# Projections of a hybrid attention and SSD layer in column-tile pairs by seven products (Strassen's scheme), token halves in turn, V in four pieces

## The chip, the cores and the metric

The kernel runs on one core of a Trainium2 chip, written in Bass with the Tile framework. The metric is the device time of one execution in microseconds (us). The engines are named as in the profile: PE (TensorE, matmuls), PEld (its weight loads), DVE (VectorE), ACT (ScalarE), POOL (GpSimd) and SP (SyncE, which here only issues DMAs).

## The reference, cut to what matters

One decoder layer over 2048 tokens of 1024 channels, in float32. One input projection feeds two branches: dilated sliding-window attention with three dilations, and a Mamba-2 SSD mixer behind a causal convolution of width 4.

```python
proj = jnp.einsum('bsd,de->bse', x, w_in[layer])          # 2048 x 1024 times 1024 x 6672
q, k, v, z_att, z_ssm, xbc, dt_raw = jnp.split(proj, list(SPLITS), axis=-1)
# three dilated windows over q, k, v, merged by their log-sum-exps
y_att = rms_norm(y_att.reshape(Bsz, S, D_ATT) * jax.nn.silu(z_att), att_norm_g[layer])
xbc = jax.nn.silu(causal_depthwise_conv(xbc, conv_w[layer], conv_b[layer]))
xs, bm, cm = jnp.split(xbc, [D_SSM, D_SSM + SSM_GROUPS * SSM_STATE], axis=-1)
# chunked scan of 16 chunks of 128 tokens over xs, bm, cm, dt
y_ssm = rms_norm(y.reshape(Bsz, S, D_SSM).astype(x.dtype) * jax.nn.silu(z_ssm), ssm_norm_g[layer])
out = jnp.einsum('bse,ed->bsd', jnp.concatenate([y_att, y_ssm], axis=-1), w_out[layer])
x = layer_norm(alpha * x + out, ln_g[layer], ln_b[layer])
```

## The kernel before, in words

Every large product keeps float32 accuracy by a split of both factors into a high part (float32r) and a low rest, and three matmuls: high times high, high times low, low times high. The split of x is made once: `load_x` brings a tile of 128 channels by 1024 tokens, ACT copies it to `xh`, DVE subtracts to get `xl`. The 32 tiles of xh and xl (8 channel blocks k, 2 token halves i, high and low) stay in SBUF through the whole first half of the kernel.

V comes first (L154 to L156). Here the tokens are the output's partitions and the columns run along the free axis, in pieces of 384, 384 and 272 columns (the last holds the 16 columns of dt as well). `load_v` loads and splits the weights of a piece, `v_out` evacuates the PSUM tile of 128 tokens into `vt` (two buffers) and stores it to DRAM in three layouts, `d_v[0]` to `d_v[2]`, one for each dilation. The first piece runs with the channel blocks outermost on eight PSUM tiles, so that it can begin while x is coming in; the other two run tile by tile, each after a column tile of z.

The rest of the projection has 44 column tiles of 128 columns, where the columns are the partitions and 512 tokens the free axis. `proj(ct, fin)` loads a tile's weights (`load_w`, split by ACT and POOL), and for each of four blocks of 512 tokens makes 8 x 3 matmuls into one PSUM tile (L111 to L113), then calls `fin`, which evacuates it: `fin_z` (SiLU, to `d_za`), `fin_qk` (high and low parts to `d_qh`, `d_ql`, `d_kh`, `d_kl`), `fin_zs` (SiLU of the SSM gate, to `d_zs`) or `conv_evac` into a tile U of all 2048 tokens, from which `conv_out` makes the convolution on DVE (L227, L229), its SiLU on ACT (L233) and the stores to `d_xs` and `d_bc`. The order: V with two tiles of z, 12 convolution tiles, the decays (dt), 8 tiles of the SSM gate with `split_w` beside them (the output weights scaled by the norm's gains, split and stored to `d_wo`), then 16 tiles of q and k and the last z tiles. Beside the q and k tiles run the 32 units of the SSD scan, `ssd(n, g)`: 16 chunks by 2 groups.

After that come attention (eight pairs of heads, on an order written out by hand) and the output projection with both norms; both read what the first half stored to DRAM. The order of instructions on each engine in the first half is made when the kernel is built, by a list scheduler with a simulated timeline; on the chip each engine takes its instructions in that order. All of SP's DMAs stand in one queue, POOL's in another. Pools opened after others were closed reuse their memory, and a tile there waits until the tiles that it overlaps are done with.

Of the kernel before, what the change touches and what calls it, by code (L numbers as in the profile page):

```python
# [9 lines left out]
F32 = mybir.dt.float32  # L10
# [18 lines left out]
def hybrid_layer(ctx, tc, xT, xc, w52, wv, convw, convb, dtb, alog, dskp, gcol, wout,  # L29
# [23 lines left out]
    d_zs = [dtile(f"d_zs{g}", [16, 128, 4, 128]) for g in range(2)]  # L53
# [21 lines left out]

    with ExitStack() as c1:
        xp = c1.enter_context(tc.tile_pool(name="xp", bufs=1))
        wp = c1.enter_context(tc.tile_pool(name="wp", bufs=2))
        ev = c1.enter_context(tc.tile_pool(name="ev", bufs=5))
        sm = c1.enter_context(tc.tile_pool(name="sm", bufs=1))  # L80
        pp = c1.enter_context(tc.tile_pool(name="pp", bufs=3, space=PSUM))
        ss = c1.enter_context(tc.tile_pool(name="ss", bufs=5, space=PSUM))
# [6 lines left out]
        xh, xl = [[None, None] for k in range(8)], [[None, None] for k in range(8)]  # L89
        for i in range(2):  # L90
            for k in range(8):
                xh[k][i] = xp.tile([128, 1024], F32R, name=f"xh{k}_{i}")
                xl[k][i] = xp.tile([128, 1024], F32R, name=f"xl{k}_{i}")

        def load_w(ct):
            raw = wp.tile([128, 8, 128], F32, name="wraw")
            nc.sync.dma_start(raw, w52[ct])
            hi = wp.tile([128, 8, 128], F32R, name="whi")
            lo = wp.tile([128, 8, 128], F32R, name="wlo")
            nc.scalar.copy(hi, raw)  # L100
            nc.gpsimd.tensor_tensor(lo, raw, hi.bitcast(F32), op=OP.subtract)  # L101
            return hi, lo

        def proj(ct, fin, w=None, tbs=range(4)):
            hi, lo = w or load_w(ct)
            for tb in tbs:
                ps = pp.tile([128, 512], F32, name="pp")
                s = slice(tb % 2 * 512, tb % 2 * 512 + 512)
                for k in range(8):
                    h, l = xh[k][tb // 2][:, s], xl[k][tb // 2][:, s]  # L110
                    nc.tensor.matmul(ps, hi[:, k, :], h, start=(k == 0), stop=False)  # L111
                    nc.tensor.matmul(ps, hi[:, k, :], l, start=False, stop=False)  # L112
                    nc.tensor.matmul(ps, lo[:, k, :], h, start=False, stop=(k == 7))  # L113
                fin(ps, tb)

        def fin_z(i):
            def f(ps, tb):
                e = ev.tile([128, 512], F32, name="ev")
                nc.scalar.activation(e, ps, AF.Silu)
                nc.sync.dma_start(d_za[i][:, tb * 512:tb * 512 + 512], e)  # L120
            return f

        def fin_qk(i, scale):
            def f(ps, tb):
                hi = ev.tile([128, 512], F32R, name="ev")
                lo = ev.tile([128, 512], F32, name="ev")
                nc.scalar.activation(hi, ps, AF.Copy, scale=scale)
                nc.vector.scalar_tensor_tensor(lo, ps, scale, hi.bitcast(F32), op0=OP.mult,
                                               op1=OP.subtract)
                s = slice(tb * 512, tb * 512 + 512)  # L130
                dh, dl = (d_kh, d_kl) if scale == 1.0 else (d_qh, d_ql)
                nc.sync.dma_start(dh[i][:, s], hi.bitcast(F32))
                nc.sync.dma_start(dl[i][:, s], lo)
            return f


        with tc.tile_pool(name="vp", bufs=1, reuse_waits="tile") as vp:
            vw = {}
            COLS = ((0, 384), (384, 384), (768, 272))

            def load_v(pc, k):
                c0, w = COLS[pc]
                vh, vl = [vp.tile([128, 384], F32R, name=f"v{p}{k}")[:, 0:w] for p in "hl"]
                raw = vp.tile([128, 384], F32, name="vraw", bufs=2)[:, 0:w]
# [13 lines left out]
            vts = {}  # L158

            def v_out(ps, pc, r, dtj=None):  # L160
                c0, w = COLS[pc]
                if pc == 2:
                    w = 256
                    nc.vector.tensor_copy(dtj[:, 16 * r:16 * r + 16], ps[:, w:w + 16])
                r4, s4 = r // 4, r % 4
                if s4 == 0:
                    vts[0] = vp.tile([128, 4, 384], F32, name="vt", bufs=2)[:, :, 0:w]
# [9 lines left out]
            pst = [pp.tile([128, 512], F32, name="pp") for _ in range(3)]  # L177
            pst += [ss.tile([128, 512], F32, name="ss") for _ in range(5)]

            def load_x(k, i):  # L180
                st = wp.tile([128, 1024], F32, name=("wraw", "whi", "wlo")[k % 3])
# [6 lines left out]
            for i in range(2):  # L188
                for k in range(8):
                    if i == 0:  # L190
                        load_v(0, k)
                    load_x(k, i)
                    for r in range(8):
                        v_mm(pst[r], 0, 8 * i + r, k)
                for r in range(8):
                    v_out(pst[r], 0, 8 * i + r)
            nc.sync.dma_start(ident, cst[:, 0:128])
            nc.sync.dma_start(tri, cst[:, 128:256])
            nc.sync.dma_start(cw, convw)
            nc.sync.dma_start(cb, convb)  # L200
            nc.sync.dma_start(dsk, dskp)
            nc.sync.dma_start(gc, gcol)

            for pc in (1, 2):
                proj(23 + pc, fin_z(pc - 1))
                for k in range(8):
                    load_v(pc, k)
                dtj = ev.tile([128, 512], F32, name="ev")[:, 0:256] if pc == 2 else None
                for r in range(NR):
                    ps = pp.tile([128, 512], F32, name="pp")  # L210
                    for k in range(8):
                        v_mm(ps, pc, r, k)
                    v_out(ps, pc, r, dtj)
            nc.sync.dma_start(d_dt.rearrange("j r h -> j (r h)"), dtj)


        def conv_evac(U, ps, tb):
            p3 = ps.rearrange("p (s j) -> p s j", j=NJ)
            evac(tb, U[:, 3 + tb:19:4, :], p3)
            if tb:  # L220
                nc.vector.tensor_copy(U[:, tb - 1, 1:NJ], p3[:, 3, 0:NJ - 1])
            else:
                nc.gpsimd.memset(U[:, 0:3, 0:1], 0.0)

        def conv_out(cp, U, i):
# [5 lines left out]
            o = cp.tile([128, 16, NR, 8], F32, name="cvo", bufs=1)  # L231
# [12 lines left out]
        with tc.tile_pool(name="cp", bufs=2, reuse_waits="tile") as cp:  # L244
            for i in range(12):
# [176 lines left out]
        for i in range(8):  # L422
            jobs += [(i, fin_qk(i, -0.125)), (8 + i, fin_qk(i, 1.0))]
# [538 lines left out]
```

## Time and profile before

| | |
|---|---|
| Time, median of 3 runs | 2191.73 us (2190.43 to 2192.97) |
| The profiled execution: time, span | 2193.83 us, 2192.0 us |
| Granted TensorE clock, mean over the span | 0.984 |
| Busy share of the span: PE, PEld, DVE, ACT, POOL | 98%, 81%, 53%, 39%, 38% |
| Bytes moved by DMA, mean rate | 363.66 MB, 166 GB/s |
| Hardware queue (SP's): MB, share of the 16 DMA engines | 278.45, 41.8% |
| Software queue (POOL's): MB, share of the 16 DMA engines | 82.84, 10.6% |

Matmuls are pipelined: each row of the profile gives one matmul's time from its start to its modelled end, which is longer than the distance from one start to the next. What a matmul costs in a full stretch is therefore read from the number of matmuls in a window, not from its mean duration. The rows of windows give, for each engine, its busy time and its number of instructions in that window, then the granted clock, the mean busy share of the DMA engines, and GB/s.

### The profile page before, as it was taken

How to read it: one execution, taken by the hardware profiler on the slowest of the kernel's cores; microseconds unless marked ns; L12 is line 12 of the kernel's file. 1: busy time of each engine (PE TensorE's matmuls, PEld its weight loads, DVE VectorE, ACT ScalarE, POOL GpSimd, SP SyncE). 2: the span in 40 equal slices, each digit the busy share in tenths (PEclk: the TensorE clock that was granted, in tenths of full speed). 3: DMA queues.
4: the chain of work that ended last, by engine and by line, in shares of the span. 5: the costliest groups of instructions: out<-in, count | busy, mean ns of one | idle time of the engine just before them, and what ended most of it. 6: DMA issues, size and time to landing. Idle time of an engine off the chain costs nothing.

```text
span 2192.0 us, 37071 instructions
## 1 busy us (share of the span) xinstructions
PE 2138.5 (98%) x13968; PEld 1784.6 (81%) x13968; DVE 1166.2 (53%) x2941; ACT 847.8 (39%) x2289; POOL 838.8 (38%) x589
## 2 busy tenths in 40 slices
PE   8999999999999999999999999999999976999998
PEld 8999888888888888888888878888878865888886
DVE  4000255555223555554544258888888845655655
ACT  4101122223112333232345368887888841222221
POOL 3101010102442455555555321776666670322322
PEclk9999999999999999999999979999999988999999
DMA  8644222224786656555543542777876799232220
GB/s 281 182 133 139 70 78 71 77 71 148 249 262 208 206 194 198 178 190 177 171 157 129 195 148 76 228 219 223 241 216 184 208 360 276 99 104 83 93 84 29
DMA packets 213955, 363.66 MB, mean 166 GB/s; under 512 B 37776, under 2 KB 125968, under 8 KB 203536
## 3 DMA queue, kind: packets, MB, share of 16 engines
q1 hardware_dynamic: 197408, 278.45, 41.8%
q0 software_dynamic: 16368, 82.84, 10.6%
q8 instruction: 110, 1.80, 0.3%
q14 instruction: 69, 0.57, 0.1%
HBM read 226.62 MB, written 134.61 MB: 165 GB/s over the span
## 4 chain that ended last, share of the span: by engine, by line
PE 89%; DMA 4%; DVE 4%; ACT 2%; SPq 1%; issue 1%; POOL 0%; DVEq 0%; POOLq 0%; ACTq 0%
PE pp L112 14%; PE pp L111 14%; PE pp L113 14%; PE N L577 6%; PE T L557 6%; PE S L528 6%; PE S L737 3%; PE S L739 3%; PE S L738 3%; PE pp L155 2%; PE pp L156 2%; PE pp L154 2%; PE T L737 2%; PE T L738 2%; PE T L739 2%; PE ss L386 1%
## 5 line engine op out<-in xcount | busy, mean ns | idle before, releaser
L111 PE MATMUL pp<-xh,whi 128*128 128x512 f32 x1408 | 550.3, 391 | 0.0
L112 PE MATMUL pp<-xl,whi 128*128 128x512 f32 x1408 | 549.6, 390 | 0.0
L113 PE MATMUL pp<-xh,wlo 128*128 128x512 f32 x1408 | 548.5, 390 | 0.0
L544 ACT ACTIVATE P<-P,st 128x256 f32<-128x256 f32 (+1 forms) x768 | 345.4, 452 | 94.7 <-DVE st L536 94.1
L113 PEld LDWEIGHTS pp<-xh,wlo 128*128 128x128 f32 x1408 | 264.3, 188 | 55.4
L111 PEld LDWEIGHTS pp<-xh,whi 128*128 128x128 f32 x1408 | 264.4, 188 | 54.7
L112 PEld LDWEIGHTS pp<-xl,whi 128*128 128x128 f32 x1408 | 264.4, 188 | 54.0
L536 DVE CUSTOM_DVE_ANT_0 P<-S,tb 128x256 f32<-128x256 f32 (+1 forms) x768 | 235.3, 362 | 107.3 <-PE S L528 76.1
L101 POOL TENSOR_TENSOR wlo<-wraw,whi 128x1024 fp32r<-128x1024 f32 x44 | 105.5, 2397 | 365.1 <-ACT whi L100 352.1
L559 DVE COPY PT<-T 128x512 f32<-128x512 f32 (+1 forms) x304 | 196.5, 677 | 2.3 <-PE T L557 2.2
L557 PE MATMUL T<-ident,P 128*128 128x128 f32 x1200 | 179.4, 286 | 6.3 <-DVE PT L559 5.9
L577 PE MATMUL N<-PT,v 128*64 128x128 f32 x2400 | 176.4, 284 | 0.0
L577 PEld LDWEIGHTS N<-PT,v 128*64 128x64 f32 x2400 | 129.2, 138 | 33.2 <-issue 22.6
L557 PEld LDWEIGHTS T<-ident,P 128*128 128x128 f32 x1200 | 129.7, 142 | 31.5 <-DVE PT L559 7.3
L544 ACT ACTIVATION_READ_ACCUMULATOR P<-P,st 128x1 f32 x768 | 144.7, 188 | 0.0
L644 POOL TENSOR_TENSOR wb<-num,wb 128x2048 f32<-128x2048 f32 x21 | 96.3, 4586 | 97.1 <-DMA wb<-d_wd 69.3
L528 PE MATMUL S<-kh,qp 64*128 64x256 f32 (+1 forms) x1024 | 126.3, 306 | 0.0
L379 DVE TENSOR_SCALAR mt<-csb,cs 128x128 f32<-128x128 f32 x256 | 75.2, 363 | 71.2 <-DMA csb<-d_cs 71.2
L714 DVE TENSOR_REDUCE tb<-P 128x128 f32<-128x1024 f32 x32 | 64.0, 2000 | 85.6 <-PE N L743 49.2
L528 PEld LDWEIGHTS S<-kh,qp 64*128 64x128 f32 x1024 | 88.8, 188 | 22.0 <-issue 20.9
L154 PE MATMUL pp<-vh,xh 128*128 128x384 f32 (+1 forms) x304 | 95.0, 320 | 6.0 <-ACT xh L184 5.4
L100 ACT CAST whi<-wraw 128x1024 fp32r<-128x1024 f32 x44 | 46.1, 1047 | 138.3 <-PE pp L112 130.5
(295 smaller groups left out, 3807.1 us busy)
## 6 DMA issues: line engine op xcount, KB each, us to landing
v<-d_v POOLq DMA_DIRECT2D x24, 1024.0 KB, 7.0
wb<-d_wd SPq DMA_DIRECT2D x48, 512.0 KB
wraw<-w SPq DMA_DIRECT2D x44, 512.0 KB
d_wo<-wot SPq DMA_DIRECT2D x32, 512.0 KB
csb<-d_cs SPq DMA_DIRECT2D x32, 512.0 KB
d_v<-vt SPq DMA_DIRECT2D x64, 192.0 KB
d_za<-ev SPq DMA_DIRECT2D x32, 256.0 KB
d_xs<-cvo SPq DMA_DIRECT2D x8, 1024.0 KB
```

The lines of the kernel that those rows point to most:

```text
L111: nc.tensor.matmul(ps, hi[:, k, :], h, start=(k == 0), stop=False)
L112: nc.tensor.matmul(ps, hi[:, k, :], l, start=False, stop=False)
L113: nc.tensor.matmul(ps, lo[:, k, :], h, start=False, stop=(k == 7))
L154: nc.tensor.matmul(ps, h, vw[k][0], start=(k == 0), stop=False)
L528: nc.tensor.matmul(ov(sp[h][:, 256 * b:256 * b + w]), A["q"][d][x][hr, blk], kv(A["k"][y][hr]), start=(m == 0), stop=(m == 2))
L536: nc.vector.tensor_tensor_reduce(P[:, h, b, 256 - w:256], sp[h][:, c0:c0 + w], tab[:, h, tab.shape[2] - w:], 1.0, 3.0e38, OP.add, OP.min, ...
L544: nc.scalar.activation(p, p, AF.Exp, bias=stat(A, 0, d, h, blk), scale=-1.0, accum_out=stat(A, 1, d, h, blk))
L557: nc.tensor.transpose(tp[:, h, b], P[:, h, b, 128 * which:128 * which + 128], ident)
L559: nc.vector.tensor_copy(pt[:, :, bl[0]:2], tp[:, :, bl[0]:2])
L577: nc.tensor.matmul(nm[64 * h:64 * h + 64, bq * 128:bq * 128 + 128], v[:, k, 64 * h:64 * h + 64], pts[which][:, h, b], start=(f or not whic ...
L737: nc.tensor.matmul(ps, uh[:, e, :], wh, start=(e == 0), stop=False)
L738: nc.tensor.matmul(ps, uh[:, e, :], wl, start=False, stop=False)
```

## The change

V is made first and alone, in four pieces of 256, 256, 256 and 272 columns, each for one half of the tokens on eight PSUM tiles, channel blocks outermost.

The 44 column tiles are taken in 22 pairs, and the tokens in two halves of 1024. For a pair and a half, the product is one of 2 x 2 blocks: two column tiles by two halves of the input channels (512 each), times two halves of the channels by two blocks of 512 tokens. It is made by Strassen's scheme in Winograd's form, from seven products of blocks: each is 4 channel blocks x 3 matmuls of 512 tokens (`products`). Three of the seven are accumulated in PSUM onto one that is still there, after ACT has copied the earlier value out (`keep`); DVE makes the four results from two partial sums each (`put`).

Four of the seven factors on the tokens' side are sums of x's blocks. `sums(p, k)`, called after the first and the second piece of V, loads x's blocks again, makes the sums on DVE, splits them on ACT and DVE, and stores them, with the three plain blocks of xh and xl, to `d_T` in DRAM: 7 factors, high and low, for both halves. `token_side(p)` loads the fourteen tiles of a half (14 x 1 MB) into SBUF through POOL's queue. The half changes twice: ten jobs (a pair in a half) on half 0, twenty-two on half 1, twelve on half 0. The tiles of the next half are loaded one after another, each after the product of the last job that used the same tile.

On the columns' side `column_side` loads a pair's weights, makes four sums on DVE and splits the seven factors on ACT and POOL; it runs one job ahead, step by step after the products of the running job.

The convolutions need all tokens: their half 0 goes to DRAM (`d_cu`) and is loaded back into U in half 1. The split of the output weights moves to the first eight jobs and its first product from POOL to ACT. The SSD units begin after job 21 and run beside 21 jobs, on single mt tiles. The SSM gate's tensor is stored as two halves.

The core of the diff:

```diff
-            COLS = ((0, 384), (384, 384), (768, 272))
+            COLS = ((0, 256), (256, 256), (512, 256), (768, 272))
...
+            def sums(p, k):
+                r = [ts.tile([128, 1024], F32, name="st", bufs=4) for _ in range(2)]
+                for h in range(2):
+                    kk = k + 4 * h
+                    nc.sync.dma_start(r[h], xT[kk * 128:(kk + 1) * 128, p * 1024:(p + 1) * 1024])
+                b11, b12, b21, b22 = r[0][:, 0:512], r[0][:, 512:1024], r[1][:, 0:512], r[1][:, 512:1024]
...
+                sub(b11, b12, b11)
+                sub(b12, b22, b12)
+                sub(b22, b22, b11)
+                sub(b21, b22, b21)
+                for t, names in zip(r, (("T1", "T3"), ("T4", "T2"))):
+                    h = ts.tile([128, 1024], F32R, name="tp", bufs=6)
+                    l = ts.tile([128, 1024], F32R, name="tp", bufs=6)
+                    nc.scalar.copy(h, t)
+                    nc.vector.tensor_tensor(l, t, h.bitcast(F32), op=OP.subtract)
+                    for a, x in enumerate((h, l)):
+                        for c, nm in enumerate(names):
+                            nc.sync.dma_start(d_T[p, nm][a][:, k], x.bitcast(F32)[:, 512 * c:512 * c + 512])
+                for nm, kk, s in (("B11", k, 0), ("B21", k + 4, 0), ("B22", k + 4, 512)):
+                    for a, x in enumerate((xh, xl)):
+                        nc.sync.dma_start(d_T[p, nm][a][:, k], x[kk][p].bitcast(F32)[:, s:s + 512])
...
+            for pc in range(4):
+                for i in range(2):
+                    pst = [pp.tile([128, 512], F32, name="pp") for _ in range(4)]
+                    pst += [ss.tile([128, 512], F32, name="ss") for _ in range(4)]
+                    for k in range(8):
+                        if i == 0:
+                            load_v(pc, k)
+                        if pc == 0:
+                            load_x(k, i)
+                        for r in range(8):
+                            v_mm(pst[r], pc, 8 * i + r, k)
                     for r in range(8):
+                        v_out(pst[r], pc, 8 * i + r)
...
+                if pc < 2:
+                    for k in range(4):
+                        sums(pc, k)
...
+        wp = c1.enter_context(tc.tile_pool(name="wp", bufs=7, reuse_waits="tile"))
+        wr = c1.enter_context(tc.tile_pool(name="wr", bufs=7, reuse_waits="tile"))
+        tp = c1.enter_context(tc.tile_pool(name="tp", bufs=1, reuse_waits="tile"))
+        ev = c1.enter_context(tc.tile_pool(name="ev", bufs=6, reuse_waits="tile"))
+        def token_side(p):
+            T = []
+            def step(nm):
+                def f():
+                    T.append([tp.tile([128, 4, 512], F32R, name=f"T{nm}{x}") for x in "hl"])
+                    for a, t in enumerate(T[-1]):
+                        nc.gpsimd.dma_start(t.rearrange("p k t -> p (k t)"),
+                                            d_T[p, nm][a].rearrange("p k t -> p (k t)"))
+                return f
+            return T, [step(nm) for nm in LEFT]
+        def column_side(ct0, ct1):
...
+            def two(src):
+                t = wp.tile([128, 2, 4, 128], F32R, name="w")
+                nc.scalar.copy(t[:, 0], src)
+                nc.gpsimd.tensor_tensor(t[:, 1], src, t[:, 0].bitcast(F32), op=OP.subtract)
+                W.append(t)
...
+        def products(W, T, fin, after, to=None):
+            def mm(ps, i, start=True):
+                w, (th, tl) = W[i], T[i]
+                for k in range(4):
+                    nc.tensor.matmul(ps, w[:, 0, k], th[:, k], start=start and k == 0, stop=False,
...
+                    nc.tensor.matmul(ps, w[:, 0, k], tl[:, k], start=False, stop=False,
...
+                    nc.tensor.matmul(ps, w[:, 1, k], th[:, k], start=False, stop=(k == 3),
...
+                for f in after[i]:
+                    f()
...
+            pa, pb, pc, pd = [pp.tile([128, 512], F32, name="pp") for _ in range(4)]
+            mm(pa, 0)
+            p1 = keep(pa)
+            mm(pb, 1)
+            put(0, 0, p1, pb, p1)
+            mm(pa, 2, False)
+            u2 = keep(pa)
+            mm(pc, 3)
+            p5 = keep(pc)
+            mm(pa, 4, False)
+            u3 = keep(pa)
+            put(1, 1, u3, p5, p5)
+            mm(pc, 5, False)
+            put(0, 1, u2, pc, u2)
+            mm(pd, 6)
+            put(1, 0, u3, pd, u3, OP.subtract)
...
+        def conv_tiles(i):
+            U = []
+            for ci in range(2):
+                u = cp.tile([128, 19, NJ], F32, name="U", bufs=2)
+                for tb in range(2):
+                    nc.sync.dma_start(u[:, 3 + tb:19:4, :],
+                                      d_cu[i + ci][:, tb].rearrange("p (s j) -> p s j", j=NJ))
...
+        conv, zs = [("c", i) for i in range(0, 12, 2)], [("s", i) for i in range(0, 8, 2)]
+        rest = []
+        for i in range(0, 8, 2):
+            rest += [("q", i), ("k", i), ("z", i)]
+        one_ = [x for i in range(4) for x in (conv[i], zs[i])]
+        jobs = [(0, x) for x in one_ + conv[4:]]
+        jobs += [(1, x) for x in one_ + [conv[4], rest[0], conv[5]] + rest[1:]]
+        jobs += [(2, x) for x in rest]
...
         for m, (ph, (kind, i)) in enumerate(jobs):
...
+            products(W, T, fin, hooks, to)
+            W, T = nW, nT
+            if ph == 0:
+                for e in range(2 * m, min(16, 2 * m + 2)):
+                    split_w(e)
...
+            upto = max(0, min(32, (m - 20) * 32 // 21))
             while done < upto:
                 ssd(*units[done])
                 done += 1
```

More of the change, by code (lines that the diff above doesn't have):

```diff
@@ L88, in hybrid_layer @@
         dsk = sm.tile([128, 8], F32, name="dsk")
[L89 to L108, printed above, removed]
-                for k in range(8):
[L110 to L114, printed above, removed]
@@ L175, in v_out @@
                                           vt[32 * n:32 * n + 32])
-            pst = [pp.tile([128, 512], F32, name="pp") for _ in range(3)]
-            pst += [ss.tile([128, 512], F32, name="ss") for _ in range(5)]
             def load_x(k, i):
-                st = wp.tile([128, 1024], F32, name=("wraw", "whi", "wlo")[k % 3])
+                st = ts.tile([128, 1024], F32, name="st", bufs=4)
                 for s in [slice(0, 512), slice(512, 1024)] if k == i == 0 else [slice(0, 1024)]:
@@ L199, in hybrid_layer @@
[L199 to L213, printed above, removed]
@@ L254, in hybrid_layer, with decays @@
         dec = sm.tile([128, 16, 16], F32, name="dec")
[L255 to L257 removed]
+        def decays(dp):
             dtbt = dp.tile([128, 16], F32, name="dtbt")
@@ new lines, in hybrid_layer @@
+        rest = []
[5 more added lines that the diff above has]
+        jobs += [(2, x) for x in rest]
+        base = {"c": 40, "s": 32, "q": 0, "k": 8, "z": 24}
+        T, steps = token_side(0)
+        W, prep = column_side(*[base[jobs[0][1][0]] + jobs[0][1][1] + i for i in range(2)])
```

262 lines of the change are left out of this document (161 added, 101 removed).

## The prediction, made before the kernel ran

> **What bounds the kernel now.** I read the page first: busy engines, the forty slices, the chain.
>
> ```profile
> span 2192.0 us, 37071 instructions
> PE 2138.5 (98%) x13968; PEld 1784.6 (81%) x13968; DVE 1166.2 (53%) x2941; ACT 847.8 (39%) x2289; POOL 838.8 (38%) x589
> ...
> PEclk9999999999999999999999979999999988999999
> DMA  8644222224786656555543542777876799232220
> ...
> PE 89%; DMA 4%; DVE 4%; ACT 2%; SPq 1%; issue 1%; POOL 0%; DVEq 0%; POOLq 0%; ACTq 0%
> ...
> L111 PE MATMUL pp<-xh,whi 128*128 128x512 f32 x1408 | 550.3, 391 | 0.0
> ```
>
> TensorE is busy 98% of the span and carries 89% of the chain. L111 and its two twins L112 and L113 make 3 x 1408 = 4224 projection matmuls with no idle time before them. Their mean of 391 ns is latency, not rate, so the next view is busy time by stretch, where the count of matmuls over a full stretch gives the spacing.
>
> ```profile
> core 0: us, PE busy (x) PEld busy (x) DVE busy (x) ACT busy (x) POOL busy (x), PEclk, DMA share, GB/s
> 5.00:35.00 30.00, 28.92 (x145) 27.65 (x146) 19.19 (x17) 19.28 (x23) 9.26 (x6) 1.00 0.95 326
> 45.00:60.00 15.00, 15.00 (x89) 15.00 (x88) 0.00 (x0) 1.03 (x2) 2.04 (x2) 1.00 0.98 288
> 110.00:160.00 50.00, 50.00 (x285) 50.00 (x284) 3.35 (x6) 2.88 (x6) 0.00 (x0) 1.00 0.49 140
> 197.00:232.00 35.00, 35.00 (x281) 35.00 (x280) 4.37 (x18) 2.24 (x6) 0.00 (x0) 1.00 0.48 135
> 275.00:495.00 220.00, 220.00 (x973) 182.15 (x972) 124.90 (x91) 48.58 (x71) 24.85 (x19) 1.00 0.24 75
> 715.00:1210.00 495.00, 495.00 (x2700) 407.86 (x2699) 252.56 (x489) 174.16 (x256) 264.20 (x187) 1.00 0.53 177
> 1245.00:1265.00 20.00, 20.00 (x90) 16.57 (x89) 0.00 (x0) 2.40 (x4) 7.24 (x11) 1.00 1.04 395
> 1270.00:1295.00 25.00, 24.76 (x162) 19.11 (x163) 11.31 (x64) 15.90 (x75) 0.00 (x0) 0.51 0.04 14
> 1755.00:1795.00 40.00, 32.73 (x320) 26.60 (x318) 20.54 (x73) 17.47 (x63) 36.17 (x21) 0.87 1.11 391
> 1785.00:1790.00 5.00, 3.26 (x8) 2.58 (x9) 0.00 (x0) 0.00 (x0) 5.00 (x8) 0.50 1.23 382
> ```
>
> Three spacings come out: a 512-wide matmul 220/973 = 0.226 us, a 384-wide 50/285 = 0.175, a 272-wide 35/281 = 0.125. Three rates of a full DMA system as well: 326 GB/s while x and the V weights come in (5 to 35 us), 288 while V's rows are written out (45 to 60), 391 to 395 where long rows are read (1245 to 1265, 1755 to 1795). In V and the projections TensorE is the bound, and the DMA engines are about half idle. That half is what the change spends.
>
> **The change, part by part.** The sum is a difference against this profiled execution (2193.83 us, its span 2192.0 and 1.83 around it), which is 2.1 us, 0.1%, above the median; I add it to the median, 2191.73.
>
> *Products.* Each pair of column tiles over half the tokens took 2 x 2 x 24 = 96 matmuls; seven products of 4 x 3 take 84. There are 22 pairs and two halves: 44 jobs, 3696 matmuls, 528 fewer. 528 x 0.226 = **-119.4 us**, all of it on the path, as L111 to L113 have no idle time. A job is now 84 x 0.226 = 19.0 us, a product 2.71.
>
> *V in four pieces.* 768 matmuls of 384 columns become 1152 of 256; 384 of 272 stay. No row has 256 columns. From 384 to 272 the spacing falls 0.0508 us in 112 columns, so 256 gives 0.125 - 0.007 = 0.117: 1152 x 0.117 against 768 x 0.175, **+0.5 us**. If 256 cost what 272 does, +9. I take the line, as 272 is so near; it can hardly be cheaper than proportional (-5).
>
> *What V must now wait for.* This is the large cost. Until the end of job 0 the DMA engines must move: x once for V and once for the sums (2 x 8.4 MB), the V weights (4.3), V in three layouts (3 x 8.4 = 25.2), the seven token operands, high and low, for both halves (14 x 2.1 = 29.4), and the seven of half 0 back in (14.7). That is 90.4 MB; the last half piece of V's writes (3.1) may come after. The operands must be written before the first job even for half 1: the ring for the columns' tiles (wp, wr) lies over the staging tiles of `sums`, and the operands' tiles (tp) over xh and xl. Without waits TensorE would end job 0 at 5.4 (its first matmul) + about 3 (slow clock, rows below) + 183 (V) + 19 = 210 us, and 87 MB in 210 us would be 415 GB/s. At the rates of the rows: reads of x and weights 21.1 MB at 326 = 65 us, writes 54.6 MB at 288 = 190, the operands' reads 14.7 at 395 = 37, less 11 for the last writes: 281; with 2 us of start and one product 285. TensorE waits 285 - 210 = **+75 us**, in V (a PSUM tile is drained to a vt of two buffers, which wait for their writes on SP's queue behind those of `sums`) and in job 0 (its operands come every 5 us or more). Low end: everything at 391 GB/s, 87.3/0.391 = 223, +18. High end: SP's queue is in order, and the stores of `sums` wait there for ACT's copies and DVE's subtractions with V's loads and stores behind them; at nine tenths of these rates 281/0.9 + 4 = 316, +106. I take the middle figure, as each part has a row of its own kind of transfer.
>
> A rule of the Trainium skill (DMA: Bandwidth & Descriptors, Specifications) says that transfers of 512 B or more run at line rate; by it 1 and 2 KB rows would cost no more than long ones, the wait would be the low end, +18, and the sum 57 us lower. The trace disagrees: V's 1.5 KB rows held 288 GB/s at a DMA share of 0.98.
>
> *Reloads.* At the change to half 1 (after 10 jobs) and back to half 0 (after 32) each operand tile is single, free when product j of the old half's last job is done and wanted one job later. The seven loads, issued on POOL's queue, take 37 us alone from 2.7 us on: the last is there at 40, wanted at 19 + 16.3 = 35: +5. With 4 MB of weights, outputs and conv inputs beside them (15 us at 288), +19. I take **+24** for both; 0 to 60. POOL's next subtractions queue behind a load that waits for its tile, but they have a job's time in hand.
>
> *Convolution in half 1, and the SSD stage.*
>
> ```profile
> L229 DVE SCALAR_TENSOR_TENSOR acc<-U,cw,acc 128x2048 f32<-128x2048 f32 x33 | 77.6, 2352 | 1.2
> L227 DVE TENSOR_SCALAR acc<-U,cw 128x2048 f32<-128x2048 f32 x12 | 41.1, 3425 | 1.3
> L233 ACT ACTIVATE cvo<-acc,cb 128x512 f32<-128x512 f32 x44 | 28.3, 715 | 61.7 <-DVE acc L229 61.7
> ...
> L111 PEld LDWEIGHTS pp<-xh,whi 128*128 128x128 f32 x574 | 107.8, 188 | 22.2
> ...
> L368 POOL TENSOR_TENSOR xde<-xdt,een 128x512 f32<-128x512 f32 x29 | 48.7, 1679 | 3.8 <-DVE xdt L357 3.8
> L101 POOL TENSOR_TENSOR wlo<-wraw,whi 128x1024 fp32r<-128x1024 f32 x18 | 43.2, 2401 | 132.8 <-ACT whi L100 132.8
> L128 DVE SCALAR_TENSOR_TENSOR ev<-pp,ev 128x512 f32<-128x512 f32 x58 | 39.9, 688 | 57.4 <-ACT ev L127 52.2 <-DMA d_kl<-ev 4.4
> L371 POOL TENSOR_TENSOR xdel<-xde,xdeh 128x512 fp32r<-128x512 f32 x29 | 37.5, 1294 | 25.8 <-ACT xdeh L370 13.9 <-DMA d_uh<-xdel 11.9
> ```
>
> Each job adds to DVE four sums of columns and four of products, 8 x 0.69 (L128) = 5.5 us; to POOL seven subtractions, 7 x 1.294 (L371, the same shape) = 9.1; to ACT seven copies and four evacuations, about 11 x 0.62 = 7 of 19 us, hidden. In half 1 the six pairs of convolutions stand in 11 jobs (209 us): DVE has 12 x (3.4 + 3 x 2.35) + 11 x 5.5 = 186 us there and waits for ACT's four SiLUs (2.9 us) before it may write the single acc again; U has two buffers, held until the result is written out. DVE at nine tenths with such waits: **+12** (0, if the four product tiles hide it, to 30). The last five rows are of the SSD stage, 715 to 1210 us: 29 units (L368) in 495 us; a unit costs POOL (264.2 - 43.2)/29 = 7.6 us. Now 21 jobs carry 32 units: POOL 32 x 7.6 + 21 x 9.1 = 434 us of TensorE's 21 x 19 + 32 x 3.7 = 517 (a unit's 3.7 is (495 - 574 x 3 x 0.226)/29), where it had 53%. At 84%, in order, some units come late: **+14** (0 to 45). The moved split of the output weights puts 25 MB beside the first eight jobs, 5.2 MB in 19 us, 275 GB/s, which the writing rate just covers: **+4** (0 to 15).
>
> *Entry to attention.* Today q is in before the last projection ends, and the scores follow at once:
>
> ```profile
> 1266.73 0.39 PE L113 MATMUL pp<-xh,wlo 128*128 128x512 f32 x1
> 1267.05 0.33 PE L528 MATMUL S<-kh,qh 64*128 64x128 f32 x2
> ```
>
> The new q tiles lie over the last job's weight tiles, free only product by product: **+5** (0 to 15). Attention and output projection are untouched.
>
> **Sum:** -119.4 + 0.5 + 75 + 24 + 12 + 14 + 4 + 5 = +15; 2191.7 + 15 = **2207 us**. Seven eighths of the matmuls is real; the traffic that buys it is dearer.
>
> **The rivals.** *The DMA engines keep up better (faster).* What decides is the mean rate over V and job 0. With the other costs as above (59 us), the wait must be under 60, so 87.3 MB in 265 us: 329 GB/s or more. The 326 of 5 to 35 us is almost there, and mixed reads and writes may overlap; the 288 speaks against, and writes are 54.6 of the 87.3 MB. At 350 GB/s the wait is 249 + 4 - 210 = 43; the same rate makes the reloads cost 10, and with DVE and POOL at half their prices 18 for the rest: -119.4 + 0.5 + 43 + 10 + 18 = -48, 2144 us. All rates at 391 and the rest as here: -119.4 + 0.5 + 18 + 10 + 18 = -73, 2119. By the Trainium skill's line-rate rule, above, it would be this one.
>
> *The clock.* A waiting TensorE is granted half the clock:
>
> ```profile
> 9.04 0.52 PE L155 MATMUL ss<-vl,xh 128*128 128x384 f32 x1
> 9.36 0.52 PE L154 MATMUL ss<-vh,xh 128*128 128x384 f32 x1
> ...
> 12.28 0.33 PE L154 MATMUL pp<-vh,xh 128*128 128x384 f32 x1
> 12.45 0.34 PE L155 MATMUL pp<-vl,xh 128*128 128x384 f32 x1
> ```
>
> After the start, spacing is 0.32 us for 7 us, then 0.17; after the gap before 1785 the clock is 0.50, and from 1270 to 1295 it stays at 0.51 with TensorE nominally busy. If V's waits were so frequent that it ran slow throughout, 256 columns would take 0.32 x 256/384 = 0.213: V 1152 x 0.213 + 384 x 0.227 = 333 us, job 0 at 360 instead of 285, 2282 us. Against it: a half piece is 192 matmuls, 22 us, without need of new data, and 7 us of slow start each are covered by the DMA. The Trainium skill (TensorE: Matmul & The Clock Gate, Part 1) gives half clock after an idle window of about 3.4 us; the trace agrees with 0.50, and by that rule it is this rival if waits recur within each half piece.
>
> *POOL becomes the bound of the SSD stage.* If its subtractions cost 1.68 us, as L368 does beside a busy DVE, POOL has 243 + 247 = 490 of 517 us, and the idle before L371 and L368 (30 us) no longer fits: +45 instead of +14, 2238 us.
>
> *Nothing moves:* the terms cancel to within 0.2% (4.4 us, about what a measurement of this kernel tells from no change).
>
> **How the numbers follow.** Chances: my forecast, slower by 5 to 50 us, 0.40; the better DMA 0.41 (0.04 of it at 391); no change 0.08; POOL 0.07; the clock 0.04. So faster 0.41, same 0.08, slower 0.51. The range goes from 2145, the better DMA's time, to 2250, above POOL's; about 0.1 lies outside at each end. The likeliest case alone is 2196 to 2245.
>
> **What would show it.** Matmuls: 3696 of 512 columns in the projections at 0.226 us apart. V: PEclk below 1 and the DMA digit at 9 through the first 280 us, waits of TensorE for vt, vh or operand tiles of about 75 us in all, job 0 ending near 285. Two gaps of about 12 us at the reloads. POOL busy near 84% in the SSD stage. Wrong: if job 0 ends before about 265 us, the V term fails; if it ends near 285 but the whole is still faster, the smaller terms do; if TensorE's waits lie in the SSD stage, it is POOL.

## The result, and the profile after

The changed kernel takes 2369.69 us (median of 4 runs, 2368.98 to 2374.02), the kernel before on the same chip 2192.35: a ratio of 1.081 (95% interval 1.080 to 1.083), 177 us slower. The forecast was slower too, but by 15 us, with a range that ended at 2250.

The page of the changed kernel:

```profile
span 2368.6 us, 39212 instructions
PE 2091.1 (88%) x13824; PEld 1721.6 (73%) x13824; DVE 1552.2 (66%) x3313; ACT 1087.8 (46%) x2771; POOL 1198.4 (51%) x871
...
PEclk8789889999999999998999996999999998899999
DMA  9996969794455565569545544467777779532220
...
PE 32%; DVE 3%; DMA 3%; issue 2%; ACT 2%; POOL 1%; SPq 0%; DVEq 0%; POOLq 0%; ACTq 0%
...
L234 POOL TENSOR_TENSOR w<-wr,w 128x512 fp32r<-128x512 f32 x308 | 479.9, 1571 | 271.8 <-ACT w L233 250.4
...
L229 DVE TENSOR_TENSOR wr<-wr 128x512 f32<-128x512 f32 x176 | 190.6, 1083 | 124.2 <-DMA wr<-w 88.4
```

TensorE has fallen from 98% of the span to 88%, and no engine has taken its place: DVE is at 66%, POOL at 51%. The shares of the chain add up to 41% only: it could be followed back from the end to 1338 us, so it tells nothing of V and little of the jobs. Two of the new lines among the costliest matter most below, and both are the columns' side of the scheme: the low parts on POOL (L234, 1571 ns each) and the sums on DVE (L229, 1083 ns each).

The rows of TensorE's timeline, with the idle time before a matmul and its releaser in brackets, give the boundaries of the stages:

```profile
299.51 0.80 PE L255 MATMUL pp<-TB11h,w 128*128 128x512 f32 x1 [18.22 <-ACT w L233]
...
1430.19 0.39 PE L259 MATMUL pp<-TB22h,w 128*128 128x512 f32 x1
1442.95 0.47 PE L675 MATMUL S<-kh,qh 64*128 64x128 f32 x2 [12.38 <-DMA kh<-d_kh]
```

The first product starts at 299.5 us, the last ends at 1431, attention starts at 1443 (before: 1267). From there to the end it is 925.7 us against 924.9: the whole loss lies ahead of attention. The timeline has 3696 matmuls of products, 84 a job, so that the end of each job can be counted off:

| stage | measured us | TensorE's own time | above it | in the forecast |
|---|---|---|---|---|
| to the start of job 0 | 299.5 | 191 | 108 | 75 with job 0 |
| job 0 | 25.7 | 19 | 7 | |
| jobs 1 to 9 (half 0) | 186.6 | 171 | 16 | 4 |
| the two jobs after a change of half | 25.8, 36.1 | 19, 30 | 13 | 24 |
| jobs 11 to 20 (convolutions, half 1) | 227.8 | 190 | 38 | 12 |
| jobs 21 to 43 (SSD units), less 6 for the reload | 659 | 437 + 32 x 3.7 = 555 | 104 | 14 |
| entry to attention | 12.4 | 0 | 12 | 5 |

The column "above" sums to 298; with -119.4 for the products and +0.5 for V that is +179, and the spans differ by 176.6. Jobs 8 and 9 run undisturbed, 19.0 us from end to end: the saving of an eighth is there. What it costs is more than twice the saving. Not all of that is idle time: over jobs 10 to 43 (512 to 1431 us, window below) TensorE was busy 811 of 919 us, so 108 us were idle; the granted clock was 0.96 there, where it was 1.00 in the kernel before from 715 to 1210 us, and 4% of 919 us is about another 37 us (an estimate).

The waits of TensorE, in total, times and longest:

```profile
PE pp L121 <- ACT vh L113: 65.3, 6, 31.5
PE pp L255 <- ACT ev L266: 37.7, 28, 4.1
PE ss L483 <- DVE mt L479: 21.2, 12, 4.3
PE pp L255 <- ACT w L233: 20.3, 2, 18.2
...
PE ss L456 <- DVE y L495: 16.3, 11, 2.6
```

In V it waits for V's own weights (vh), 65 us in six places, 53 of them after x is in (three waits from 80 to 183 us); then 18 us for the first job's weights; in the jobs in many small pieces for DVE's results or for ACT's copies out of PSUM (L266). ACT, in its turn, waited for DVE: 80.8 us for mt (L476) and 67.0 us for ev (L274).

### The profile page after: what moved, and what is told of

It is laid out like the page before. It is cut to its first block, busy times and chain, and to the rows that moved or that the text cites. A ratio compares the mean times of both kernels' runs of the same rounds, so it can differ in the third digit from the quotient of the medians.

```text
span 2368.6 us, 39212 instructions
## 1 busy us (share of the span) xinstructions
PE 2091.1 (88%) x13824; PEld 1721.6 (73%) x13824; DVE 1552.2 (66%) x3313; ACT 1087.8 (46%) x2771; POOL 1198.4 (51%) x871
## 2 busy tenths in 40 slices
DMA packets 283189, 482.04 MB, mean 204 GB/s; under 512 B 45808, under 2 KB 153456, under 8 KB 267376
## 5 line engine op out<-in xcount | busy, mean ns | idle before, releaser
L234 POOL TENSOR_TENSOR w<-wr,w 128x512 fp32r<-128x512 f32 x308 | 479.9, 1571 | 271.8 <-ACT w L233 250.4
L229 DVE TENSOR_TENSOR wr<-wr 128x512 f32<-128x512 f32 x176 | 190.6, 1083 | 124.2 <-DMA wr<-w 88.4
L233 ACT CAST w<-wr 128x512 fp32r<-128x512 f32 x308 | 186.7, 617 | 125.9 <-PE pp L259 62.5
L266 ACT COPY ev<-pp 128x512 f32<-128x512 f32 x176 | 102.1, 581 | 71.4 <-PE pp L259 60.3
L121 PE MATMUL pp<-vh,xh 128*128 128x256 f32 (+1 forms) x256 | 70.4, 303 | 71.3 <-ACT vh L113 65.3
L114 POOL TENSOR_TENSOR vl<-vraw,vh 128x256 fp32r<-128x256 f32 (+1 forms) x32 | 33.6, 1058 | 190.1 <-ACT vh L113 190.1
L476 DVE TENSOR_SCALAR mt<-csb,cs 128x128 f32<-128x128 f32 x256 | 108.6, 492 | 3.7 <-PE ss L483 2.4
L121 PEld LDWEIGHTS pp<-vh,xh 128*128 128x128 f32 x256 | 48.8, 204 | 73.0 <-ACT vh L113 66.5
L355 DVE SCALAR_TENSOR_TENSOR acc<-U,cw,acc 128x2048 f32<-128x2048 f32 x36 | 101.4, 2816 | 0.4
L923 POOL TENSOR_TENSOR kh<-kh,wb 128x1024 f32<-128x1024 f32 x8 | 19.2, 2400 | 142.9 <-DVE kh L922 142.9
```

Of the source, the lines that this page charges most:

```text
L121: nc.tensor.matmul(ps, h, vw[k][0], start=(k == 0), stop=False)
L229: tt = lambda o, a, b, op=OP.subtract: nc.vector.tensor_tensor(o, a, b, op=op)
L233: nc.scalar.copy(t[:, 0], src)
L234: nc.gpsimd.tensor_tensor(t[:, 1], src, t[:, 0].bitcast(F32), op=OP.subtract)
```

## The experiments

Two theories had to be told apart from their rivals: in V, bytes against the order of SP's queue; in the jobs, DVE slowed by POOL against POOL, or DVE's own load, as the bound. The differences are against the changed kernel's 2369.69 us. Only the complete kernel near the end was executed four times, the other runs once, and the changed kernel's own four executions lie 5 us apart. A new kernel also gets a new static order, so a difference of a few us is not read.

**Fewer bytes in V.**

```diff
-                if pc < 2:
+                if pc < 1:
...
-                                            d_T[p, nm][a].rearrange("p k t -> p (k t)"))
+                                            d_T[0, nm][a].rearrange("p k t -> p (k t)"))
```

> Leaves out the token sums of half 1 and their stores (18.9 MB of DMA in the V stage); half 1's jobs read half 0's operands instead. Theory DMA: V and the start of job 0 (299.5 us in the changed kernel) are paced by bytes, 306 GB/s over the first 300 us, so 18.9 MB fewer bring job 0 forward by 18.9/0.306 = 62 us, to about 238, and the time from 2369 to about 2307. Rival, order and drains: TensorE waits in V because SP's queue is in order and because of the slow clock; then the start of job 0 moves by less than 30 us and the DMA share in the first 240 us falls clearly below 0.9.

2335.94 us, 34 less. Job 0 starts at 261.8, 38 us earlier: between the two theories. The DMA share to 240 us is 0.85, below 0.9 as the rival had it. Bytes are a part of it; something else gives 24 of the 62 us back. The windows of the changed kernel (us, then busy time and count of PE, PEld, DVE, ACT, POOL, granted clock, DMA share, GB/s) point to it:

```profile
0.00:200.00 200.00, 129.23 (x968) 127.61 (x969) 72.19 (x85) 50.53 (x78) 27.98 (x31) 0.82 0.95 313
200.00:240.00 40.00, 39.16 (x324) 38.96 (x324) 1.70 (x4) 4.19 (x12) 8.39 (x12) 1.00 0.74 214
240.00:300.00 60.00, 34.37 (x249) 33.94 (x248) 4.87 (x24) 3.90 (x10) 5.73 (x11) 0.80 1.02 344
```

To 200 us the DMA engines are full, with x, the token sums and V's first stores, while TensorE is at two thirds; then TensorE is full and the DMA engines are not; then the operands and first weights come in, the engines full once more and TensorE waiting. The two resources take turns. SP's queue suggests why, and the next run tries it: the stores of the sums (L171) and their loads (L157) stand ahead of V's next weights (L112), and the first job's weights (L225) behind all of V's stores (L137 to L141):

```profile
95.78 7.81 SPq L171 DMA_DIRECT2D d_T0T<-tp  x12
103.63 1.92 SPq L157 DMA_DIRECT2D st<-xT  x3
105.65 1.14 SPq L112 DMA_DIRECT2D vraw<-wv  x2
...
291.49 3.01 SPq L141 DMA_DIRECT2D d_v<-vt  x4
294.54 0.44 SPq L199 DMA_DIRECT2D d_dt<-dtj  x1
295.03 1.89 SPq L225 DMA_DIRECT2D wr<-w  x4
```

**V's weights past the queue.**

```diff
-                nc.sync.dma_start(raw, wv[:, k, c0:c0 + w])
+                nc.gpsimd.dma_start(raw, wv[:, k, c0:c0 + w])
```

> V's weights are loaded through POOL's queue; SP's queue keeps the rest. Theory queue order: TensorE's 65 us of waits for vh come from loads that stand in SP's queue behind the stores of the token sums; now V's pieces run early, beside these stores, and job 0 starts 20 to 35 us earlier, at 265 to 280, with the DMA share at 0.95 or more until then. Theory bytes: the 90 MB need their 290 us whatever the order: job 0 moves by less than 10 us, and the wait goes from vh to vt or to the operands.

2347.91 us, 22 less; job 0 starts at 276.3, V ends at 254 instead of 281. The order was worth 23 us of the wait; the waits for vh after x is in fall from 53 to 20 us, and the wait for the first job's weights grows from 18 to 22. To 240 us the DMA engines now stay full at 329 GB/s:

```profile
0.00:240.00 240.00, 186.18 (x1424) 184.55 (x1425) 74.66 (x101) 56.27 (x94) 56.16 (x81) 0.90 0.98 329
```

**The first job's weights past the queue.**

```diff
-        def column_side(ct0, ct1):
+        def column_side(ct0, ct1, eng=nc.sync):
...
-                    nc.sync.dma_start(t, w52[ct][:, 4 * h:4 * h + 4, :])
+                    eng.dma_start(t, w52[ct][:, 4 * h:4 * h + 4, :])
...
-        W, prep = column_side(*[base[jobs[0][1][0]] + jobs[0][1][1] + i for i in range(2)])
+        W, prep = column_side(*[base[jobs[0][1][0]] + jobs[0][1][1] + i for i in range(2)], eng=nc.gpsimd)
```

> Only the first job's weights are loaded through POOL's queue instead of SP's, where they stand behind V's last stores (loaded from 295 us in the changed kernel, TensorE waits 18.2 us for them). Theory queue order: job 0 starts 12 to 18 us earlier, at 282 to 288, and the time falls to about 2353. Theory bytes: the DMA engines are full then (331 GB/s from 250 to 300 us), so the weights only take the place of other bytes: under 6 us.

2359.74 us, 10 less. Job 0 starts at 285.4, 14 us earlier, as the queue theory had it, but ends only 9 us earlier (316), and jobs 1 to 9 take 6 us more, so that job 9 ends 3 us earlier: most of the wait moves on. The 10 us come for the most part from another place, the entry to attention, which takes 2.7 us in this order instead of 12.4.

**No reloads.**

```diff
-                if ph2 != ph:
+                if False:
```

> Leaves out both reloads of the token operands (29.4 MB); half 1 is computed from half 0's operands. The job after the first change took 25.8 us and after the second 36.1 us, where 19 and about 30 are usual: my account of the trace gives the reloads 6.8 + 6 us, so the time falls by 10 to 16 us, to about 2356. The prediction's term was 24 us. If the reloads also slow other work by their traffic, more than 24 us go.

2352.76 us, 17 less. The two jobs take 19.0 and 29.6 us: 13 us by these, the amount read from the trace; the entry to attention, 3.1 us instead of 12.4, adds to the time that is gone. The forecast's 24 was too much.

**No sums of the columns' blocks.**

```diff
-                tt(s1, a21, a22, OP.add)
-                tt(a21, a11, a21)
...
-                tt(a11, s1, a11)
-                tt(a12, a12, a11)
...
-            return W, [first, second] + [lambda t=t: two(t) for t in (a11, s1, a21, a12, a22)]
+            return W, [first, second] + [lambda t=t: two(t) for t in (a11, a22, a21, a12, a22)]
```

> Leaves out the four sums of the columns' blocks on DVE (190.6 us busy in the changed kernel, 1083 ns each); the seven products use plain blocks. Theory DVE: in the jobs from 512 to 1430 us DVE, with its load and its slowing beside POOL, is what TensorE waits for. There 34 jobs lose 4 x 1.1 to 1.25 us of DVE, about 145 us of 710 busy; of the 154 us that these jobs take above TensorE's own time at least 60 go: 2310 or less. Rival POOL (it holds the seven low parts, 75% busy): little changes, 2340 to 2370. V and job 0 stay as they are in both.

2312.56 us, 57 less: jobs 10 to 20 take 235.7 us instead of 253.6, jobs 21 to 43 625 instead of 665. DVE counts, just short of what was expected. The edit also drops the tile s1, so that a job takes four of the seven wr buffers instead of five; how much of the gain is due to that, no run tells.

**No low parts on POOL.**

```diff
-                nc.gpsimd.tensor_tensor(t[:, 1], src, t[:, 0].bitcast(F32), op=OP.subtract)
...
-                    nc.tensor.matmul(ps, w[:, 1, k], th[:, k], start=False, stop=(k == 3),
+                    nc.tensor.matmul(ps, w[:, 0, k], th[:, k], start=False, stop=(k == 3),
```

> Leaves out the seven low parts of the columns' factors on POOL (479.9 us busy); the third matmul uses the high part again. Theory contention: DVE's operations with both operands in SBUF are slowed while POOL works (column sums 673 ns at least, 1083 in the mean, 1817 at most), so without POOL's work the column sums fall to about 0.75 us, the convolution's steps from 2.82 to 2.35, and 60 to 110 us go: 2260 to 2310. If POOL itself were the bound, the same gain but DVE's durations stay. If only DVE's own load counts, 2340 to 2370.

2245.24 us, 124 less, more than any theory had. Jobs 10 to 20 take 219, jobs 21 to 43 584, attention follows the last job at once. DVE's column sums fall from 1083 to 776 ns, the convolution's steps from 2816 to 2346. In the window of its jobs 10 to 43 DVE does as many instructions as in the changed kernel (888 and 887) in 554 us instead of 713 (the changed kernel's row is shown further down):

```profile
507.00:1310.00 803.00, 772.55 (x3921) 630.88 (x3920) 553.83 (x888) 431.44 (x719) 248.02 (x214) 0.99 0.67 219
```

That speaks for contention, but POOL's result is also out of the chain that leads to a product. Two more runs look at this.

**The low parts made, but not waited for.** Only the matmul's operand changes (the second edit above); POOL does all its work.

> POOL still makes all seven low parts, but the third matmul uses the high part, so that no product waits for POOL's result; POOL's work and its neighbourhood to DVE stay. Contention theory (POOL's work slows DVE's): the time stays near the changed kernel's, 2340 to 2370, and DVE's column sums keep 1.0 to 1.1 us. Rival (TensorE waits for the low parts, a chain ACT, POOL, TensorE in each job): the time falls to that of the kernel that leaves the low parts out, 2245 to 2280.

2372.07 us: nothing is gained, and the column sums take 1092 ns. It is not that products wait for POOL's results; it is that POOL works. One other link is left in this run: DVE's column sums wait for wr tiles that POOL still reads, 30.9 us in 24 waits (34.2 us in the changed kernel). No run takes that away and leaves the slowing.

**The low parts on DVE.**

```diff
-                nc.gpsimd.tensor_tensor(t[:, 1], src, t[:, 0].bitcast(F32), op=OP.subtract)
+                nc.vector.tensor_tensor(t[:, 1], src, t[:, 0].bitcast(F32), op=OP.subtract)
```

> Computes everything; moves the seven low parts from POOL to DVE. Load theory: DVE gets 7 x 0.69 = 4.8 us more in each job (44 jobs, 213 us), is over 90% busy from 512 to 1430 us, and the time rises by 50 to 120 us: 2420 to 2490. Contention theory: with POOL free of the weights DVE's other operations lose about 0.4 us each (some 25 in an SSD job), which pays for the added ones: 2340 to 2390.

2296.47 us, 73 less, below even the contention theory's figure, with the same arithmetic and 308 more instructions on the busier engine. DVE's lines in this kernel, and its window over jobs 10 to 43 beneath that of the changed kernel (same jobs; the count of DVE's instructions is the number behind its busy time):

```profile
L234 DVE TENSOR_TENSOR w<-wr,w 128x512 fp32r<-128x512 f32 x308 | 244.7, 805 | 83.4 <-ACT w L233 81.1 <-PE ss L457 2.1
L229 DVE TENSOR_TENSOR wr<-wr 128x512 f32<-128x512 f32 x176 | 135.1, 768 | 39.1 <-DMA wr<-w 35.3 <-issue 2.2
```

```profile
512.00:1431.00 919.00, 811.29 (x3922) 646.89 (x3920) 712.64 (x887) 428.48 (x717) 631.19 (x441) 0.96 0.56 188
```

```profile
506.00:1351.00 845.00, 786.73 (x3897) 636.46 (x3895) 713.46 (x1113) 432.39 (x717) 249.79 (x204) 0.97 0.61 204
```

DVE does 1113 instructions in the 713 us in which it did 887. The 226 added ones took about 226 x 0.805 = 182 us, so about as much had been lost to POOL's neighbourhood; the direct count of the run without the low parts, 713 less 554, gives 159. Which of DVE's operations lose is seen in the durations (min/median/max, ns) of one line of the changed kernel in its two forms, with the second operand in PSUM (pp) and with both in SBUF:

```profile
L274 DVE TENSOR_TENSOR ev<-ev,pp x114: 626/675/689, 307.5 to 1430.6; 128x512 f32<-128x512 f32 x114
...
L274 DVE TENSOR_TENSOR ev<-ev x38: 677/810/1812, 320.6 to 1428.6; 128x512 f32<-128x512 f32 x38
```

With an operand in PSUM never above 689; with both in SBUF from 677 to 1812. The longest exceeds the shortest by 1135 ns, less than one of POOL's subtractions (1261 at least). The timeline shows what such an operation waits for. Here is one of the column sums, with the instruction of POOL that was under way when it began:

```profile
1366.83 1.76 DVE L229 TENSOR_TENSOR wr<-wr 128x512 f32<-128x512 f32 x1 [2.94 <-POOL w L234]
```

```profile
1366.75 1.30 POOL L499 TENSOR_TENSOR y<-y,zt 128x512 f32<-128x512 f32 x1
```

POOL's ends at 1368.05, DVE's 0.54 us later. Of the 176 column sums, 86 began while an arithmetic instruction of POOL was under way. Of these, 83 took 797 to 1817 ns and ended 545 to 559 ns after that instruction; three took no longer than usual. The other 90 took at most 694 ns. The Trainium skill (SBUF — State Buffer, SBUF: two separate sides) describes this: DVE and GpSimd share one pair of SBUF ports, a DVE operation with two SBUF inputs takes it as an exclusive lock against a GpSimd operation that reads SBUF, and the loser waits for the whole instruction. The trace agrees, with 689 ns at most where one input is in PSUM and up to 1812 where both are in SBUF; the prediction had not drawn on that page. It is not only operations with two operands in SBUF that lose: the convolution's small copies from SBUF to SBUF, with one operand, took 872 ns in the mean and 221 once the low parts are off POOL. This is their line in the changed kernel and in the one with the low parts on DVE:

```profile
L346 DVE COPY U<-U x24: 209/724/3315, 518.1 to 768.9; 128x127 f32<-128x127 f32 x24
```

```profile
L346 DVE COPY U<-U x24: 214/221/229, 512.6 to 733.7; 128x127 f32<-128x127 f32 x24
```

**All suspects out.** The edits of the first token-sum run, of the two runs on the columns' side, of the first weights, and `range(1, 2)` for `range(1, 4)` in the convolution's later taps.

> Leaves out the suspects together: half 1's token sums, the columns' sums, the columns' low parts and two of the convolution's three later taps; loads the first weights by POOL's queue. The seven products stay, 3696 matmuls. If the account is whole, TensorE's own time comes through after V: job 0 starts near 245 us, jobs 1 to 9 take 175, 10 to 20 215, 21 to 43 565, entry 5, then 925 for the rest: about 2150, 40 us under the kernel before. If something else holds the jobs (the clock, the DMA traffic, the order of the units), it stays above 2195.

2182.51 us, 7 below the kernel before timed beside it (2189.47); the account had 2150. Jobs 1 to 9 take 178, 10 to 20 217.5, 21 to 43 574, all within 10 us of what was written. V is half of the missing 32 us: job 0 starts at 258.3 instead of 245, and ends at 280 instead of 264; the jobs are most of the other half. So the eighth of the matmuls comes through once DVE and POOL are out of the way, and V's stage alone then takes back most of it.

**A better kernel, complete.** Low parts on DVE, V's and the first weights by POOL's queue.

> Computes everything: the low parts on DVE, V's weights and the first job's weights through POOL's queue. If the three causes are separate, their gains add: 73 (low parts) + 22 (V's weights) + 10 (first weights, once more a part of the 22 us wait that is left): job 0 starts at 255 to 262, jobs 1 to 9 take 180, 10 to 20 218, 21 to 43 627, and the time is 2250 to 2270, still above the kernel before: ratio about 1.03. If bytes bound V whatever the order, it is 2280 or more.

2254.44 us (ratio 1.030, 1.028 to 1.031): 115 us better than the change, still 3% slower than before. Job 0 starts at 268.6, a little later than expected; jobs 1 to 9 take 177, 10 to 20 219, 21 to 43 619, the entry 19. V now fills the DMA engines to the end:

```profile
0.00:268.00 268.00, 201.88 (x1536) 198.96 (x1536) 76.92 (x113) 57.47 (x99) 60.10 (x89) 0.89 0.99 333
```

**The same with fewer bytes.** The edit of the first run on top.

> The three moves (low parts on DVE, V's and the first job's weights through POOL's queue) with half 1's token sums left out as well (18.9 MB; half 1 reads half 0's operands). With V's weights no longer behind the sums' stores, bytes are what is left: the 54 us of 18.9/0.33 should come out whole, where the same bytes gave 38 us with SP's order: job 0 starts at 212 to 222 instead of 269, the time is about 2204. If order or drains still hold V, job 0 starts at 235 or later.

2229.93 us; job 0 starts at 236.0, 33 us earlier instead of 54, so, as the expectation had it, order or drains still hold a part of V:

```profile
0.00:100.00 100.00, 74.45 (x566) 73.64 (x567) 43.80 (x50) 34.61 (x51) 29.48 (x41) 0.90 0.96 313
100.00:220.00 120.00, 109.07 (x889) 108.24 (x888) 9.83 (x28) 13.96 (x35) 27.70 (x45) 0.97 0.85 273
```

From 100 to 220 us TensorE is at 91% and the DMA engines at 85%: with these bytes out both are nearly full, and V's own 183 us of matmuls, which must run before the last operands have room, come next. That last reading was not tried by itself. None of these kernels with all its work beats the kernel before.

## Why the prediction was wrong

- **Products and V's pieces: right.** 3696 matmuls at 0.226 us (84 in 19.0 us), the half pieces of V that run undisturbed take 22.7 us for 192 matmuls, 0.118 each.
- **V's wait: the bytes were right, the place of the wait was not, 115 us (to the end of job 0) for 75, above the high end of 106.** 306 GB/s over the first 300 us are 92 MB. That this rate came out as in the sum (87.3 MB in 283 us, 308) is partly luck: full, the DMA engines moved more (329 to 333 GB/s in the runs that kept them full), and from 200 to 240 us they stood at 0.74. The step that failed is the sum itself: it laid the transfers end to end and took TensorE's work to fit in beside them. It looked for the wait at vt and at job 0's operands; by the profile TensorE waited 8 us for vt and never for an operand of job 0, but 65 us for vh and 18 for the first weights. In the static order the stores of the sums held up V's weights, so that TensorE's work came after the transfers instead of under them (23 us by the run that moved these loads), and the first weights stood behind V's last stores (14 us at the start of job 0, of which 3 were left at the end of job 9). The high end had the stores of the sums ahead of V's loads, but as a tenth off the rates. With both loads moved (and the low parts on DVE), job 0 ends at 291, near the 285 of the forecast. Job 0 itself took 7 us too long, at a clock of 0.86: the matmuls were 0.43 us apart or more until 303.6 us, after the wait of 18.2 us, and again from 310.3 to 313.6, after a wait of only 2.1 us (the prediction spoke of about 3.4). Over the first 200 us the clock was 0.82 in the mean. The rival of the clock named this. That it is not the main cost is argued, not tried: the DMA engines were 95% busy up to 200 us, so a faster TensorE would have had to wait for them.
- **Reloads: right in kind, too dear,** 13 for 24.
- **Convolution and SSD stage: the step that failed worst, 142 us for 26.** This is the price of DVE's added work (8 x 0.69 us in a job) and, with it, DVE's load. The prediction priced DVE's new work with L128's 0.69 us, an operation that reads PSUM, and took POOL's added time as a matter of POOL's share alone. The column sums have both operands in SBUF and took 1.08; q's and k's low parts, which in the new kernel read SBUF, took 1.27 instead of 0.69; the convolution's steps 2.82 instead of 2.35. With all that DVE was 78% busy over jobs 10 to 43, in order, and TensorE waited in small pieces. Leaving out POOL's low parts took 115 us off jobs 10 to 43, while letting POOL make them for nobody took none off; moving them to DVE, which then had to make them, still took 74. So POOL's work beside DVE, with the wait for its wr tiles, is most of the 142, and the rest was not tried by itself. The rival "POOL becomes the bound" saw the neighbourhood (L368's 1.68) from the wrong side: POOL's slowing, not DVE's; POOL was busy 484 of 665 us in the SSD jobs, 73%, where the forecast had 84%. The kernel before showed it already, in rows that the prediction did not use: one line of DVE with both operands in SBUF, from the SSD stage where POOL works, and one from the convolutions, where POOL is nearly idle (29 of 248 us). The spread is the sign:

```profile
L382 DVE TENSOR_TENSOR mt<-mt,cbm x32: 1212/2420/3190, 699.6 to 1228.8; 128x1024 f32<-128x1024 f32 x32
```

```profile
L229 DVE SCALAR_TENSOR_TENSOR acc<-U,cw,acc x36: 2350/2352/2354, 263.2 to 507.3; 128x2048 f32<-128x2048 f32 x36
```

- **Jobs 1 to 9:** 16 for 4; waits for evacuations and weights while the DMA engines were busy, not tried by itself. With the low parts off POOL these jobs took 180 us instead of 187. **Entry to attention:** 12 for 5; TensorE waited for k (12.4 us), not for q as I had argued, and in runs with a new order it was between 0 and 19.
- **The line-rate rival** (everything at 391 GB/s): the kernel that kept the DMA engines full had 333 GB/s over 268 us, writes of 1 and 2 KB rows being the larger part. That rival is out, though no run tells the length of the rows from the direction of the transfer; its neighbour at 329 to 350 had the rate right and still not the time.

## What to carry to other kernels

Price an added operation by a row with the same operands in the same memories and with the same neighbours at work: a two-operand addition or subtraction in SBUF cost 0.67 to 0.69 us undisturbed and up to 1.82 beside POOL. Work on the "less busy" engine can slow the busier one; moving it over to that one gained 73 us here. A saving on the bound engine that is bought with traffic (118 MB more here: 482.04 against 363.66) has to be checked against the order of the queue that carries it, not against its free share: loads that the bound engine needs next must not stand behind stores that are needed only later.

## What the runs showed of the hardware that I had not expected

That DVE loses some 160 to 180 us over jobs 10 to 43 to POOL's low parts beside it, above all in operations with both operands in SBUF, some in copies from SBUF to SBUF, and nothing in those with one operand in PSUM. That 83 of the 86 column sums that began beside an instruction of POOL ended some 550 ns after that instruction, wherever in it they began. That with DVE at 78%, POOL at 69% and ACT at 47% over jobs 10 to 43, TensorE still lost 142 us. That a wait of 2.1 us was followed by 3 us of matmuls at about half the rate. And a DMA system that is full with mixed loads and stores moved 329 to 333 GB/s for 240 us and more, well above the 288 of V's stores and below the 391 of long reads.
